# RWKV mixer: the planner counts TensorE's operands as ready 0.3 later than their end

## The chip, the cores and the metric

One NeuronCore of a Trainium2 chip runs the whole program. The metric is the device time of one execution in microseconds; of the kernel before three runs are shown. TensorE is called PE here, VectorE DVE, ScalarE ACT, GpSimd POOL, and SP is the queue that issues most DMAs. PE's granted clock is either 1.00 (2.4 GHz) or 0.50 (1.2 GHz) in the profile.

## What is computed

A trunk of two layers over 256 tokens of width 2048, in float32. Layer 0 is attention plus a Mamba-2 mixer, layer 1 an RWKV-7 mixer, and each is followed by a squared-ReLU MLP. The change touches layer 1's mixer alone. Cut to what matters:

```python
r = xr @ w_r;  k = xk @ w_k;  v = xv @ w_v            # 2048 x 2048 each
a = sigmoid(a0 + (xa @ a1) @ a2);  g = sigmoid(xg @ g1) @ g2
def step(S, inp):                                     # one head, one token
    r_t, w_t, k_t, v_t, a_t, b_t = inp
    sa = einsum('bhvk,bhk->bhv', S, a_t)
    S = S * w_t[:, :, None, :] + sa[..., None] * b_t[:, :, None, :] + v_t[..., None] * k_t[:, :, None, :]
    return S, einsum('bhvk,bhk->bhv', S, r_t)
y = group_norm(y) * ln_w + ln_b + bonus;  out = (y * g) @ w_o
```

## The kernel before

**Layout.** Activations stand with channels on the 128 partitions and the 256 tokens along the free axis. A projection of 2048 to 2048 is cut into 16 output tiles of 128 (units), each over 16 k tiles. For accuracy each weight tile is split into a rounded part hi (ACT) and a rest lo (DVE), so that one k tile costs three matmuls on PE: hi with the rounded input, hi with the input's rest, lo with the rounded input. The text calls these three a **triple**. In the order of PE's instructions a triple is two rows, `pu<-S?,hi ... x2` and `pu<-S?,lo`, with SA or SB as the input.

**The RWKV mixer** (`mixer1`) runs over 16 pairs of heads. The recurrence is done in four chunks of 64 tokens, and each pair is a set of stages, each a chain of short steps over PE, DVE, ACT and POOL:

- `prep_a` (PE: `ps_a`, the low-rank products) and `prep_b` (PE: `ps_b`) make the scaled keys and queries; small transfers (`dn`, `Nb`) spread diagonal blocks, and `substitute` inverts them on POOL.
- `values` reads a unit of the projection v out of its PSUM bank (PE: `pu<-rk`, `pu<-cst,v`). The bank is free for the next unit only after that. There are two such banks.
- `levels` builds an inverse of 64 by 64 from those of 16: four PE steps, `ps_i<-X,NT`, `ps_i<-Pm,Xt`, `ps_i<-X,NT`, `ps_i<-Xt,P`, each of which needs what DVE (or ACT) made of the one before.
- `chunks` carries the state over four chunks. In each, PE does `ps_c<-uv,AR`, then DVE copies `rhs`, PE does `ps_c<-rhs,YY`, ACT writes `uv`, PE does `ps_c<-uv,bkn` and `ps_y<-uv,G`, and DVE updates the state for the next chunk.
- `finish` normalises on DVE and POOL, transposes on PE (`ps_y<-cst,yc`), and `mixed` splits the result on ACT and DVE into SB (pairs 0 to 7) or SA (pairs 8 to 15), the input of the output projection.

**What sets the order.** Every engine executes its instructions in the order written. A planner in the kernel's Python, the class `Streams`, writes that order: it holds every stage and the feed of projections (`load`, `halve`, `project` in `feed`) as sequential programs, knows a rough duration of each operation, and issues next the operation that can start first. `start` (L238) computes that: for PE it is the later of the time when PE is free and the time when the operands are there, plus the load of the first stationary operand. A triple of the projection has its operands long before, so it can start whenever PE is free. The feed issues its parts in a fixed list; the last are four parts that need the mixed heads: three with SA (units `+0`, `+1`, `+2` of the output projection, where k tile 15 needs pair 15) and one with SB. After `mixer1` comes `out_proj`, written in plain order, which does the rest of the output projection. SP issues the weights' loads, three tiles ahead, and the small transfers, and its order comes from the same planner.

Of the kernel before, what the change touches and what calls it, by code (L numbers as in the profile page):

```python
# [6 lines left out]
F32R = mybir.dt.float32r  # L7
# [6 lines left out]
P = 128  # L14
# [11 lines left out]
# ---------------------------------------------------------------- host layout  # L26

# order of the 64 channels of a rotary head: each 32-partition quadrant holds 16
# frequencies of the first half followed by the same 16 of the second half
ROPE = np.concatenate([np.arange(0, 16), np.arange(32, 48), np.arange(16, 32), np.arange(48, 64)])  # L30
# query heads of an output tile: one of an even and one of an odd key/value head
# [50 lines left out]
for _k, _v in CONST.items():  # L82
    _l = int(_k in ("triu", "cos", "sin", "amask"))     # the second array serves layer 0 alone
    COFF[_k] = (_l, NCONST[_l], _v.shape[1])
    NCONST[_l] += _v.shape[1]


def _units(w):
    """[K, M] -> [M/128, 128, K/128, 128]"""
    k, m = w.shape  # L90
    return np.ascontiguousarray(w.reshape(k // P, P, m // P, P).transpose(2, 1, 0, 3))
# [6 lines left out]
def _heads(v):  # L98
    """a column to a head, on the first 64 partitions"""
    return np.concatenate([v.reshape(-1, HD).T, np.zeros((HD, D // HD), np.float32)], 0)  # L100


def layout(inp):
# [7 lines left out]
        np.arange(3584, 4096),            # B, C  # L111
        np.arange(2560, 3584),            # x
        np.arange(1280, 1536), kcols,     # v, k
        qcols,
        np.arange(1536, 2560),            # z
# [43 lines left out]
# ---------------------------------------------------------------- interleaving  # L159
# [4 lines left out]
def eP(cost, after=None, shape=WIDE):  # L164
    """shape: the time to load the first stationary operand, which the matmul before hides, and the
    last matmul's time, which hides the next load"""
    return "P", cost, after, shape
# [22 lines left out]
# the order of the parts of the projections and the weights by which Streams chooses  # L190
# [5 lines left out]
def prm(n, d):  # L196
    return PRM.setdefault(n, d)


class Streams:  # L200
    count = -1
    """Issues the operations of several sequential programs in one order for every engine.

    A program is a generator; before an operation it yields the engine, a rough duration (us) and the
    time its operands are there (default: when its last operation ends), or the events it has to
    follow (which no later operation of it starts before). The operation that can start first is
    issued next."""
    LAT = {"P": 0.2, "D": 0.13, "A": 0.15, "G": 0.1, "S": 2.3}

    def __init__(self):  # L210
# [7 lines left out]
        self.dma = 0.0  # L218

# [15 lines left out]
    def stream(self, g, bias=0.0, lasting=False):  # L235
        """lasting: may still run when run() returns"""
        self.heads.append([g, None, 0.0, bias, 0.0, lasting])

    def start(self, h):
        """when the operation at the head of a program can start"""  # L240
# [9 lines left out]
        if op[0] == "P":  # L250
            load = op[3][0]
            return max(self.free["P"] + max(0.0, load - self.tail), t + load - 0.07)
        return max(self.free[op[0]], t)

    def transfer(self, t, n):
        """when a load of n columns that could end at t at the earliest ends"""
# [3 lines left out]
    def run(self):  # L260
        """until the programs that aren't lasting are done"""
# [27 lines left out]
class Part:  # L289
    """Some k tiles of a unit, a 128-wide output tile of a projection. tiles: where the halves of the  # L290
    weights come to stand if the feed shall only split them; ready: the events that X[:, k] (the tiles) wait for"""
# [5 lines left out]
class Turns:  # L297
    """Tiles of a pool, n to a name, in turn"""
# [11 lines left out]
# ---------------------------------------------------------------- the program  # L310

class Trunk:
# [4 lines left out]
    # -- small helpers ---------------------------------------------------  # L317
# [34 lines left out]
    def split(self, dst, src):  # L352
        """dst F32R [.., 512]: the rounded value and what it leaves, exactly"""
# [3 lines left out]
    def rsqrt(self, pool, v, shape, tag):  # L357
        """v f32 SBUF (any compact shape) -> 1/sqrt(v), Newton from the exponent trick"""
# [11 lines left out]
    # -- a 128-wide output tile of x @ W: [128, 512] in PSUM, the sum of its  # L370
    #    two halves is the product ------------------------------------------
# [20 lines left out]
    # -- 1/rms of the tokens --------------------------------------------------  # L392
# [8 lines left out]
    def token_rstd(self, acc, n, out_bc, pspool, tag):  # L401
        """acc: squares summed over tiles [128 ch, 256]; -> 1/rms [128 t, 2], and on all partitions in out_bc"""
# [17 lines left out]
    # -- projections as streams -------------------------------------------  # L420
    def even(self, t):
        """whether Pool should take what could start at t"""
# [3 lines left out]
    def feed(self, sch, parts, pool=None, step=1, bias=(0.1, 0.0), also=(), lasting=False):  # L426
        """Loads, splits and multiplies parts in their order. A unit's product stands in sums[unit] at
        ("sum",) + unit, and its reader has to set ("out",) + unit; parts with tiles of their own end with
        ("w", key) and their reader sets ("used", key). pool(t): whether Pool takes the low halves, step: k tiles
        issued at once; both can be changed in sch. also: (i, event, tile, source), loads behind the one of part i"""  # L430
# [77 lines left out]
    # -- squared-ReLU MLP ------------------------------------------------------  # L508
    def norm_split(self, k, x, gname, X):
        """X[:, k] = split(x * g)"""  # L510
# [4 lines left out]
    def mlp(self, l, x, X, U, acc, finish, end=NK):  # L515
        """end: the output tiles from there on lack the last quarter of the hidden units"""
# [21 lines left out]
    # -- layer 0: attention and SSD ---------------------------------------------  # L538
    def rsqrt_steps(self, pool, v, tag):
        """rsqrt as steps of a stream"""  # L540
# [15 lines left out]
    def rstd_steps(self, acc, n, out_bc, pspool, pool, tag):  # L556
        """token_rstd as steps of a stream, from several partial sums"""
# [20 lines left out]
    def mixer0(self, x, X, Y, early):  # L578
        """early: the output tiles to which the attention heads are added ahead of the SSD heads"""
# [3 lines left out]
        with tc.tile_pool(name="m0", bufs=1) as m0, tc.tile_pool(name="m0t", bufs=1) as mt, \  # L583
# [9 lines left out]
            # the projections, in the order of their use  # L593
# [6 lines left out]
            # the input goes between the first weights, the constants behind it  # L600
# [5 lines left out]
            # the norm of the input  # L606
# [12 lines left out]
            def squares(k):  # L619
                """on ACT and DVE or on Pool, a sum to each"""  # L620
# [50 lines left out]
            def steps(_):  # L671
                """the time steps, their decays and the sums of those"""
# [15 lines left out]
                # softplus = max(v, 0) + log1p(exp(-|v|)), log1p(e) = 2 atanh(e / (2 + e))  # L688
# [38 lines left out]
            # B, C, x: causal convolution, SiLU  # L727
# [25 lines left out]
            # SSD  # L753
# [7 lines left out]
            def shared(_):  # L761
                """what the heads of a group share"""
# [72 lines left out]
            # attention  # L835
# [5 lines left out]
            def rope(dst, u, n=None, ns=None):  # L841
                """n: the weights of a norm, ns: with its halves exchanged"""
# [17 lines left out]
            def heads(j):  # L860
                """values and keys, then queries"""
# [52 lines left out]
            def attn(i, j):  # L914
# [34 lines left out]
                # the transposed probabilities, normalised  # L949
# [26 lines left out]
            # the gate and its group norm  # L976
# [52 lines left out]
    def out_proj(self, w, Y, x, finish, part=None, early=NK, ahead=0):  # L1029
        """part: what the first half of the rows of w has given (all of them for the first ahead tiles); it is in x  # L1030
        already for the first early tiles"""
# [12 lines left out]
    # -- layer 1: RWKV-7 time mixing ---------------------------------------------  # L1044
# [677 lines left out]
```

## Time and profile before

| | us |
|---|---|
| runs | 2529.85, 2542.24, 2548.86 (median 2542.24) |
| profiled execution, span (the page gives no other time of it) | 2551.5 |
| PE busy over the span | 2477.5 (97%) |
| DVE busy | 1738.2 (68%) |
| ACT busy | 1306.5 (51%) |
| POOL busy | 527.2 (21%) |
| HBM traffic over the span | 162 GB/s |
| the pairs of heads, 1320 to 1761 us: span, PE busy | 441.00, 424.64 |

Busy time is the union of an engine's instructions. For PE it is a modelled end, so a busy PE can still run at half its clock; the granted clock of a stretch has to be read beside it. A wait that a row of the timeline shows in brackets is time in which the engine stood still before the instruction, and the name behind the arrow is what it waited for.

### The profile page before, as it was taken

To read this page: it belongs to the slowest core of one execution; us is meant where nothing else is said; L and a number is where in the kernel's file an instruction comes from. 1 tells how busy PE (TensorE), PEld (TensorE's weight loads), DVE (VectorE), ACT (ScalarE), POOL (GpSimd) and SP (SyncE) were. 2 spreads that over 40 slices of the span, in tenths; PEclk is the share of its full clock that TensorE was granted. 3 is DMA by queue.
4 is the path that set the end of the run, shared out by engine and by line. 5 is a ranking of instruction groups with operands and counts; after the bars stand their busy time and mean duration, and the time that the engine had idled before them with its cause. 6 is when DMAs were issued, how large, how long until landed. Compare 5 with 4: busy or idle time off the path is not lost. (4 is left out here: it accounts for less than half of the span.)

```text
span 2551.5 us, 45990 instructions
## 1 busy us (share of the span) xinstructions
PE 2477.5 (97%) x17612; PEld 2181.3 (85%) x17612; DVE 1738.2 (68%) x3287; ACT 1306.5 (51%) x2398; POOL 527.2 (21%) x933
## 2 busy tenths in 40 slices
PE   8999999999999999979999999999899999999999
PEld 7988988888888888879998888788688888888887
DVE  7888876656656656679876767667665565665665
ACT  5455555435445345556656566555453453453543
POOL 3443200000000000046455656552200000000000
PEclk9999999999999999989999999899999999999999
DMA  5433455555555555634442323334455555555554
GB/s 193 141 108 109 151 187 182 187 185 188 184 189 184 188 184 188 209 113 164 162 153 93 108 95 106 97 108 171 145 190 186 187 184 188 185 188 185 189 194 162
DMA packets 130348, 415.27 MB, mean 163 GB/s; under 512 B 23600, under 2 KB 26288, under 8 KB 130128
## 3 DMA queue, kind: packets, MB, share of 16 engines
q1 hardware_dynamic: 128160, 406.44, 46.9%
q0 software_dynamic: 1968, 5.90, 0.6%
q8 instruction: 138, 2.26, 0.3%
q14 instruction: 82, 0.67, 0.1%
HBM read 407.56 MB, written 4.72 MB: 162 GB/s over the span
## 5 line engine op out<-in xcount | busy, mean ns | idle before, releaser
L322 DVE TENSOR_TENSOR lo<-wt,hi 128x1024 fp32r<-128x1024 f32 (+2 forms) x895 | 937.4, 1054 | 529.6 <-ACT hi L319 511.8
L319 ACT ACTIVATE hi<-wt 128x1024 fp32r<-128x1024 f32 (+2 forms) x945 | 813.6, 873 | 818.3 <-PE pu L343 786.7
L343 PE MATMUL pu<-SA,hi 128*128 128x512 f32 (+2 forms) x4184 | 1162.0, 349 | 18.2 <-ACT SA L319 8.0
L343 PE MATMUL pu<-SB,hi 128*128 128x512 f32 (+2 forms) x3304 | 1003.1, 366 | 4.0 <-POOL SB L322 2.2
L343 PE MATMUL pu<-SA,lo 128*128 128x256 f32 (+1 forms) x3168 | 895.8, 283 | 0.3 <-DVE lo L322 0.3
L343 PEld LDWEIGHTS pu<-SA,hi 128*128 128x128 f32 (+1 forms) x4184 | 724.8, 191 | 135.2 <-ACT hi L319 9.7
L343 PE MATMUL pu<-SB,lo 128*128 128x256 f32 x2752 | 775.7, 282 | 1.7 <-DVE lo L322 1.6
L343 PEld LDWEIGHTS pu<-SB,hi 128*128 128x128 f32 (+1 forms) x3304 | 587.0, 190 | 115.6 <-POOL SB L322 2.6
L343 PEld LDWEIGHTS pu<-SA,lo 128*128 128x128 f32 (+1 forms) x3168 | 603.6, 191 | 1.2 <-DVE lo L322 0.5
L343 PEld LDWEIGHTS pu<-SB,lo 128*128 128x128 f32 x2752 | 522.6, 190 | 2.5 <-DVE lo L322 2.3
L1694 POOL DMA_DIRECT2D out<-xT x16 | 8.7, 544 | 708.0 <-DVE xT L322 708.0
L1661 POOL DMA_DIRECT2D xd<-xh x13 | 7.2, 554 | 696.5 <-DVE xh L322 696.5
L322 DVE TENSOR_TENSOR xh<-xh,pu 128x256 f32<-128x256 f32 x164 | 69.2, 422 | 53.7 <-PE pu L343 51.1
L322 DVE TENSOR_TENSOR xT<-xT,pu 128x256 f32<-128x256 f32 x154 | 64.8, 421 | 47.9 <-PE pu L343 45.3
L322 POOL TENSOR_TENSOR lo<-wt,hi 128x512 fp32r<-128x512 f32 (+1 forms) x50 | 69.1, 1387 | 66.3 <-ACT hi L319 62.2
L322 POOL TENSOR_TENSOR xt<-Nb,X 128x60 f32<-128x60 f32 (+14 forms) x240 | 74.7, 311 | 28.4 <-DMA Nb<-dn 12.1
L322 POOL TENSOR_TENSOR X<-X,xt 128x60 f32<-128x60 f32 (+14 forms) x240 | 74.2, 309 | 16.4
L319 ACT ACTIVATE uv<-ps_c,n 64x64 f32<-64x64 f32 x128 | 39.5, 309 | 53.0 <-PE ps_c L343 40.3
L322 POOL TENSOR_TENSOR SB<-st,SB 128x256 fp32r<-128x256 f32 x44 | 49.3, 1135 | 43.8 <-ACT SB L319 31.4
L340 DVE SCALAR_TENSOR_TENSOR uw<-u,rb 128x256 f32<-128x256 f32 x128 | 54.5, 425 | 4.4
L340 DVE SCALAR_TENSOR_TENSOR st<-dx,vec,xh 128x256 f32<-128x256 f32 x80 | 53.3, 700 | 2.0 <-POOL SB L322 2.0
L322 DVE TENSOR_TENSOR u<-pu,eb 128x256 f32<-128x256 f32 x128 | 53.6, 418 | 0.0
(310 smaller groups left out, 2073.2 us busy)
## 6 DMA issues: line engine op xcount, KB each, us to landing
wt<-in_w_up SPq DMA_DIRECT2D x256, 512.0 KB
wt<-in_w_dn SPq DMA_DIRECT2D x256, 512.0 KB
wt<-in_w_in SPq DMA_DIRECT2D x64, 512.0 KB
wt<-in_w_out SPq DMA_DIRECT2D x32, 512.0 KB
wt<-in_w_k SPq DMA_DIRECT2D x32, 512.0 KB
wt<-in_w_v SPq DMA_DIRECT2D x32, 512.0 KB
wt<-in_w_o SPq DMA_DIRECT2D x32, 512.0 KB
wt<-in_w_r SPq DMA_DIRECT2D x26, 512.0 KB
```

The source lines that it names most:

```text
L319: return self.nc.scalar.activation(out=out, in_=in_, func=func, **kw)
L322: return (eng or self.nc.vector).tensor_tensor(out=out, in0=a, in1=b, op=op)
L340: return self.nc.vector.scalar_tensor_tensor(out=out, in0=a, scalar=s, in1=b, op0=op0, op1=op1)
L343: return self.nc.tensor.matmul(out, lhsT, rhs, start=start, stop=stop)
L1661: spill = lambda d, e=nc.gpsimd: e.dma_start(out=xd[:, d, :], in_=x[d])
L1694: store = lambda d: nc.gpsimd.dma_start(out=ap["out"][:, d, :], in_=x[d])
```

## The change

`start` adds a new attribute `slack` to the time at which a PE operation's operands count as there. It is 0.0 when the planner is made, and 0.3 (the planner's unit is a rough us) from the start of `mixer1`. Nothing is computed in another way: the same instructions are issued in another order. The diff also drops comments and texts in quotes, and one added line shifts the line numbers (L343 becomes L344). Its core:

```diff
@@ class Streams @@
         self.tail = WIDE[1]
         self.dma = 0.0
+        self.slack = 0.0
...
         t = h[2] if op[2] is None else max(op[2], h[4])
         if op[0] == "P":
             load = op[3][0]
-            return max(self.free["P"] + max(0.0, load - self.tail), t + load - 0.07)
+            return max(self.free["P"] + max(0.0, load - self.tail), t + load - 0.07 + self.slack)
         return max(self.free[op[0]], t)
...
@@ mixer1 @@
                 sch.stage(whole, self.ahead)
+                sch.slack = 0.3
                 sch.pool, sch.step, sch.bias = (...)
                 sch.run()
```

What it does to the order, on PE, at three places.

**Place 1**, the third pair, from `ps_c<-uv,bkn` of its first chunk to `ps_c<-uv,AR` of its second. Before:

```order
L343 MATMUL ps_c_12608<-uv_11961,bkn_12467 64x64 x2
L343 MATMUL ps_y_12607<-uv_11961,G_12468 64x64 x2
L343 MATMUL pu_236<-SB,hi_164 128x256 x2
L343 MATMUL pu_236<-SB,lo_165 128x256
L343 MATMUL pu_236<-SB,hi_164 128x256 x2
L343 MATMUL pu_236<-SB,lo_165 128x256
L343 MATMUL ps_c_12608<-uv_11961,AR_11796 64x64 x2
```

Now, on PE at the same place:

```order
L344 MATMUL ps_c_12613<-uv_11958,bkn_12471 64x64 x2
L344 MATMUL ps_y_12612<-uv_11958,G_12472 64x64 x2
L344 MATMUL pu_119<-SA,hi_126 128x256 x2
L344 MATMUL pu_119<-SA,lo_127 128x256
L344 MATMUL pu_119<-SA,hi_126 128x256 x2
L344 MATMUL pu_119<-SA,lo_127 128x256
L344 MATMUL pu_119<-SA,hi_126 128x256 x2
L344 MATMUL pu_119<-SA,lo_127 128x256
L344 MATMUL pu_236<-SB,hi_164 128x256 x2
L344 MATMUL pu_236<-SB,lo_165 128x256
L344 MATMUL ps_c_12613<-uv_11958,AR_11796 64x64 x2
```

Between two steps of a chain there are four triples where there were two.

**Place 2**, the 14th pair, from the second step of `levels` on. On PE before:

```order
L343 MATMUL ps_i_12480<-Pm_12472,Xt_12471 32x32 x16
L346 MATMUL pu_236<-cst,v_11962 64x128 x4
L343 MATMUL ps_b_11960<-AR_11797,bk_11909 128x128 x4
L343 MATMUL ps_i_12480<-X_12470,NT_11799 32x32 x8
L343 MATMUL pu_119<-SB,hi_164 128x256 x2
L343 MATMUL pu_119<-SB,lo_165 128x256
L343 MATMUL pu_119<-SB,hi_164 128x256 x2
L343 MATMUL pu_119<-SB,lo_165 128x256
L343 MATMUL ps_i_12480<-Xt_12471,P_12555 32x32 x8
L343 MATMUL pu_236<-SB,hi_239 128x256 x2
```

Now, on PE, up to the first steps of `chunks` of that pair:

```order
L344 MATMUL ps_i_12474<-Pm_12465,Xt_12464 32x32 x16
L344 MATMUL ps_y_12612<-uv_11958,G_11956 64x64 x2
L344 MATMUL ps_i_12474<-X_12463,NT_11799 32x32 x8
L344 MATMUL pu_236<-rk_11939,rkb_11961 128x256
L344 MATMUL ps_i_12474<-Xt_12464,P_12559 32x32 x8
L347 MATMUL pu_236<-cst,v_11959 64x128 x4
L344 MATMUL ps_c_12613<-uv_12196,AR_11795 64x64 x2
L344 MATMUL ps_c_12613<-rhs_12621,YY_11802 64x64 x2
L344 MATMUL pu_236<-SB,hi_239 128x256 x2
```

No triple is left between these steps: the projections have run on to the point where they need the PSUM bank that `values` (`pu_236<-rk`, `pu_236<-cst,v`) has to clear first. With the rows ahead of it this run has 21 rows of the mixer without a triple; there is one more such run, of 12 rows, at the first chunks of the second pair.

**Place 3**, the end: pair 15's last step of `chunks`, its transposes, and the first output unit that needs it. On PE before (21 triples stand between the first and the second row of the mixer):

```order
L343 MATMUL ps_y_12864<-uv_12199,G_11959 64x64 x2
L343 MATMUL pu_236<-SB,hi_164 128x256 x2
L343 MATMUL pu_236<-SB,lo_165 128x256
...
L343 MATMUL pu_236<-SB,lo_127 128x256
L346 MATMUL ps_y_12864<-cst,yc_12859 64x128 x4
L343 MATMUL pu_236<-SB,hi_126 128x256 x2
```

Now, on PE:

```order
L344 MATMUL pu_119<-SA,lo_165 128x256
L344 MATMUL ps_y_12892<-uv_12196,G_11956 64x64 x2
L347 MATMUL ps_y_12892<-cst,yc_12906 64x128 x4
L344 MATMUL pu_119<-SA,hi_164 128x256 x2
L344 MATMUL pu_119<-SA,lo_165 128x256
```

The 21 triples ahead of the transposes and the nine behind them have moved to earlier places; the `pu_119<-SA` row behind the transposes is already k tile 15 of unit `+0`, which needs pair 15 to be mixed.

## Rows read from the trace of the kernel before

**Rows 1.** The page: span of the profiled execution.

```profile
span 2551.5 us, 45990 instructions
```

**Rows 2.** Busy time by stretch: PE, PEld, DVE, ACT, POOL (instructions), granted clock, DMA share, GB/s.

```profile
1320.00:1761.00 441.00, 424.64 (x4914) 362.71 (x4912) 310.02 (x928) 262.38 (x659) 257.55 (x623) 0.95 0.34 110
...
1320.00:1370.00 50.00, 48.21 (x565) 41.72 (x564) 30.85 (x91) 26.80 (x67) 32.08 (x88) 0.90 0.40 119
1370.00:1420.00 50.00, 47.78 (x559) 40.75 (x560) 37.25 (x113) 29.02 (x75) 30.18 (x64) 0.93 0.32 103
1420.00:1470.00 50.00, 47.46 (x557) 40.26 (x556) 35.17 (x109) 27.76 (x70) 33.96 (x86) 0.93 0.30 97
...
1620.00:1670.00 50.00, 47.14 (x497) 39.43 (x495) 34.20 (x107) 25.74 (x64) 24.79 (x57) 0.80 0.28 89
```

**Rows 3.** PE's waits, 1320 to 1761: total us, times, longest.

```profile
PE ps_i L343 <- DVE Pm L322: 3.0, 4, 1.4
PE ps_i L343 <- DVE P L1502: 3.0, 4, 1.0
```

**Rows 4.** PE's timeline, waits in brackets: start, us, instruction; last, one stretch.

```profile
1328.05 0.45 PE L343 MATMUL ps_i<-X,NT 32*32 32x32 f32 x32 [1.24 <-DVE X L1473]
...
1330.18 0.65 PE L343 MATMUL ps_i<-Pm,Xt 32*32 32x32 f32 x32 [0.44 <-DVE Pm L322]
...
1384.44 0.34 PE L343 MATMUL ps_c<-uv,AR 128*64 128x64 f32 x4 [0.80 <-DVE uv L337]
...
1622.80 0.45 PE L343 MATMUL ps_i<-Pm,Xt 32*32 32x32 f32 x32 [0.52 <-DVE n L337]
...
1624.98 0.44 PE L343 MATMUL ps_i<-X,NT 32*32 32x32 f32 x16 [0.47 <-DVE X L322]
...
1627.71 0.44 PE L343 MATMUL ps_i<-Xt,P 32*32 32x32 f32 x16 [0.96 <-DVE P L1502]
...
1629.24 0.63 PE L346 MATMUL pu<-cst,v 128*64 128x128 f32 x4 [0.53 <-DVE bv L322]
...
1630.00:1650.00 20.00, 20.00 (x111) 16.83 (x108) 8.18 (x25) 8.05 (x21) 9.63 (x32) 0.50 0.16 46
```

**Rows 5.** PE's timeline: the steps of one pair that did not wait.

```profile
1657.79 0.45 PE L343 MATMUL ps_i<-Pm,Xt 32*32 32x32 f32 x32
...
1659.44 0.44 PE L343 MATMUL ps_i<-X,NT 32*32 32x32 f32 x16
...
1660.71 0.44 PE L343 MATMUL ps_i<-Xt,P 32*32 32x32 f32 x16
...
1662.17 0.33 PE L343 MATMUL ps_c<-uv,AR 64*64 64x64 f32 x4
...
1663.33 0.33 PE L343 MATMUL ps_c<-rhs,YY 64*64 64x64 f32 x4
```

**Rows 6.** PE's timeline at the mixer's end, and tile lo there: PE, PEld, DVE.

```profile
1748.34 0.34 PE L343 MATMUL ps_y<-uv,G 128*64 128x64 f32 x4
...
1756.27 0.60 PE L346 MATMUL ps_y<-cst,yc 128*64 128x128 f32 x4
...
1760.78 0.85 PE L343 MATMUL pu<-SA,hi 128*128 128x256 f32 x2 [0.69 <-ACT SA L319]
...
1748.70:1756.27 7.57, 5.79 (x21) 4.03 (x21) 3.77 (x6) 0.00 (x0) 1.00 1.00 364
```

**Rows 7.** PE's timeline: a triple behind a mixer step, then one behind a triple.

```profile
1716.70 0.51 PE L343 MATMUL pu<-SB,hi 128*128 128x256 f32 x2
...
1717.17 0.40 PE L343 MATMUL pu<-SA,hi 128*128 128x256 f32 x2
...
1717.52 0.40 PE L343 MATMUL pu<-SA,hi 128*128 128x256 f32 x2
```

**Rows 8.** Busy time by stretch: the output projection's start.

```profile
1761.00:1830.00 69.00, 57.61 (x330) 48.88 (x330) 50.10 (x96) 32.07 (x54) 18.85 (x12) 0.98 0.42 145
```

## Prediction, written before the changed kernel ran

> **What bounds the kernel now.** I read the page first for the span [rows 1], then busy time by stretch for the only stretch whose order changes, then PE's waits in it, then PE's timeline around them. The pairs of heads take 441.00 us, 17% of the span, and PE is busy for 424.64 us of it [rows 2]. So PE is the bound there, and the same matmuls are issued before and after. The stretch can shorten only by what PE loses in it, and there are two losses. PE stands still for 441.00 - 424.64 = 16.4 us, in 28 waits. Nearly all are for DVE, in `levels` and `chunks` [rows 3], and none names a DMA. And its clock is granted at 0.90, 0.93, 0.93 and 0.80 in four of the 50 us stretches [rows 2]: 5.0 + 3.5 + 3.5 + 10.0 = 22.0 us lost. Everything that the change can give lies in these 38 us, 1.5% of the span. What it can take away is not bounded so.
>
> **The change, part by part.** The planner now puts a triple ahead of a mixer step whose operands would come within 0.3 after PE is free. Counted in both orders over the 208 gaps between successive steps of `levels` and of `chunks`, 359 triples stood in them and 437 stand there now.
>
> *Waits between steps.* The first two waits (1.24 and 0.44 us) stand at a place where the order is nearly as it was, so they stay; the last (0.69) belongs to the end [rows 4, 6]. That leaves 25 waits and 16.4 - 2.4 = 14.0 us, 0.56 each. Place 1 shows the best case: its 0.80 us wait [rows 4] gets two more triples, 0.71 us at 0.35 each [rows 7]. But one wait in three has no more cover than before, for instance the 0.96 us one [rows 4]. The planner's 0.3 on each would be 25 x 0.3 = 7.5 us. The ends are 0 (DVE's own queue, with the weights' lo in it, makes the operands late and they stay late) and 14.0. I take -7.5, half way, since the added triples per gap (0.375 x 0.35 = 0.13 us) are few but most stand at the gaps that waited.
>
> *Two runs of mixer steps without a triple.* Here the projections wait for a PSUM bank, so DVE's time is bare. At place 2, from the second step of `levels` to the first of `chunks`, 1657.79 to 1662.17 = 4.38 us passed where PE never waited [rows 5], so the chain needs at most that when DVE is free. PE has six steps there now, at 0.33 to 0.45 us each [rows 5], some 2.1 us: up to 2.3 us idle. The next step followed after 1.16 us [rows 5]; one step of 0.33 covers it: 0.8 more. That is 3 us for the lower end. Where DVE was loaded, 1622.80 to 1629.24 = 6.44 us went by [rows 4]: 2.1 more. The steps ahead of it and the shorter run at the second pair I put at 0 to 3 together, an estimate by the waits of 0.5 to 0.96 [rows 4]. Ends 3 and 8.2; I take +6, nearer the loaded row, since DVE is busy 70% of the stretch [rows 2].
>
> *The end.* Before, from the last `ps_y<-uv,G` to k tile 15 of unit `+0`, 1748.34 to 1760.78 = 12.44 us pass, and 30 triples hide all but 0.69 of it [rows 6]. Now nothing stands there but the transposes. Less the two PE steps' own 0.34 and 0.60, 11.5 us are bare. DVE spends 3.77 us of that on lo halves [rows 6], which the new order issues ahead of or behind the chain; part of this fell while ACT or POOL had the chain, so I take half off: 9.6 us idle. The wait that was there goes: +8.9. Ends: all the lo off (+7.0), none off (+10.8). Nothing behind it makes this good: `out_proj` cannot split more than three weight tiles ahead, and PE is already idle for 69.00 - 57.61 = 11.4 us of its first 69 [rows 8].
>
> *Changes between triples and mixer steps.* A triple behind a mixer step takes 1717.17 - 1716.70 = 0.47 us, one behind a triple 0.35 [rows 7]. The projections stand in 225 runs where there were 237: 12 x 0.12 = -1.4 us, 0 to -1.4.
>
> *The clock.* The 0.50 stretch from 1630 follows four waits of 0.47 to 0.96 us within 7 us [rows 4]. Of the four losses the first follows the two waits that stay, so I keep 5.0. Of the other 17.0 I let half go with half of the waits: -8.5, between 0 and -17.0. Place 2 gets a stretch of its own: +3.5 like the 0.93 rows, 0 to 10 like the 0.80 row [rows 2]. The idle end adds one too, in a stretch where PE is busy 83% [rows 8]: +3, 0 to 6. Together -2.0. Beside this rule of thumb from rows stands one of the Trainium skill (TensorE: Matmul & The Clock Gate, section Why this matters for your kernels): it asks for no long PE-idle gap between bursts of matmuls if the clock is to hold mid-kernel. This trace does not bear that out, as no wait ahead of the 1630 stretch is over 0.96 us; by that rule the sum would be the third rival's.
>
> *Nothing for the rest.* Loads and small transfers on SP, and steps on ACT and POOL, change places by a few rows. DMA is busy 0.34, ACT 262 and POOL 258 of 441 us [rows 2], so there is room; if `substitute` on POOL came late, `levels` would be next, and that is in the waits' ends. The MLPs' order is unchanged.
>
> **Sum:** -7.5 + 6 + 8.9 - 1.4 - 2.0 = **+4.0 us**. The profiled execution, 2551.5 us, would be 2555.5; it lies 0.4% above the median of the runs, which I move by the same amount: 2542.2 + 4.0 = **2546**. The gain is real, but the order takes its cover from the end, where it hid twelve microseconds.
>
> **Rivals.** 1 (faster): the waits nearly vanish (-12), and with them the three later clock losses (-17.0) while no new one comes; the uncovered places cost their lower ends (3 and 7.0). -12 + 3 + 7.0 - 1.4 - 17.0 = -20.4: 2522. For it: clock losses are larger than waits here. Against it: eight or more us idle at the end have not been seen to pass without a loss of clock in this stretch.
>
> 2 (slower): the bank at place 2 decides. If DVE is loaded there, its 8.2 us bring a stretch at 0.50 as long as that from 1630 (+10), the end costs 10.8 and 6 of clock, and the waits, shortened by 3 only, keep their clock losses: -3 + 8.2 + 10.8 - 1.4 + 16 = +30.6: 2573. It decides from about 6 us of idle there. Against it: the waits would have to keep most of their length though 78 triples stand between the steps.
>
> 3: the clock does not answer to short waits, only to the long idle at the end. Then no loss is spared and one is added (+6): -7.5 + 6 + 8.9 - 1.4 + 6 = +12: 2554. For it stands only the skill's rule named above; the trace speaks against it.
>
> 4: the change moves rows but not waits. DVE works its queue in order, so a late operand stays late behind a lo, and the triple only shifts which step waits: 0 + 6 + 8.9 - 1.4 - 2.0 = +11.5: 2554. For it: eleven of the thirteen kinds of wait name DVE. Against it: PE would have 0.13 us more work per gap on the mean.
>
> **How the numbers follow.** About 1% (25 us) is what a measurement of this kernel tells from no change. Chances: forecast 0.62, rival 1 0.12, rival 2 0.09, rival 3 0.10, rival 4 0.07. Faster by over 1% (under 2517) needs rival 1 and a little more: 0.03, and 0.01 from the forecast's edge: 0.04. Slower by over 1% (above 2568): two thirds of rival 2 and 0.01 of the others: 0.07. Within 1%: 0.89. The range takes in the forecast with its bounds and rivals 3 and 4, and leaves out most of rivals 1 and 2: 2527 to 2563.
>
> **What would show it.** Right: PE's waits named Pm, P, uv and X fall to about half in total; one wait of 5 to 7 us ahead of the last `ps_y<-cst,yc` and one of about 4 us for SA behind it; waits at the 14th pair's `levels` that add up to 4 us or more; a granted clock below 1.00 right behind the end. Wrong: no wait over 3 us at the end, which would mean that my reading of the order there is false; or the waits between steps undiminished (rival 4); or a clock of 1.00 from the third pair on (rival 1).

## The result, and the profile after

The changed kernel took 2556.9 us (median of 13 runs, 2545.5 to 2564.3), the kernel before 2539.2 (13 runs, 2527.4 to 2549.8): a ratio of 1.0061 with a 95% interval of 1.0039 to 1.0083, or some 15.5 us more by the means of the runs (the medians lie 17.7 apart). That is slower, and less than the 1% that was set as the bound. The forecast had the sign, the range and the case (within 1%); its +4.0 was too small by 11 us, and the section on why shows that one of its terms had the wrong sign.

The page of the kernel after, for [rows 1]: its span and its engines' busy time.

```profile
span 2562.6 us, 45974 instructions
PE 2476.5 (97%) x17612; PEld 2179.5 (85%) x17612; DVE 1741.9 (68%) x3287; ACT 1308.4 (51%) x2398; POOL 534.9 (21%) x933
```

PE is busy as long as before (2477.5) and the span is 11.1 us longer: PE stands still. Busy time by stretch of the kernel after, with the columns of [rows 2]:

```profile
1320.00:1370.00 50.00, 46.86 (x669) 39.29 (x667) 34.44 (x99) 28.49 (x72) 30.99 (x83) 1.00 0.36 110
1370.00:1420.00 50.00, 48.11 (x511) 41.82 (x508) 40.38 (x118) 32.02 (x80) 36.69 (x81) 1.00 0.36 108
1420.00:1470.00 50.00, 48.46 (x589) 40.89 (x589) 37.39 (x108) 30.47 (x77) 31.58 (x74) 1.00 0.34 108
1470.00:1520.00 50.00, 47.82 (x528) 40.88 (x526) 33.28 (x101) 27.19 (x69) 24.65 (x59) 0.83 0.28 91
...
1620.00:1670.00 50.00, 45.87 (x548) 39.03 (x548) 37.71 (x113) 30.90 (x77) 31.17 (x69) 0.90 0.34 109
...
1720.00:1770.00 50.00, 40.17 (x437) 33.95 (x437) 27.52 (x83) 25.96 (x66) 17.54 (x40) 0.92 0.40 138
```

The first three stretches, which before ran at 0.90 to 0.93, are at 1.00 now; lower clocks have come later, from 1470 on and at the end. These are single executions, and run 6 below shows how far the clock moves between two of the same kernel. PE's waits in the kernel after, 1320 to 1775 (total us, times, longest), for [rows 3]:

```profile
PE ps_y L347 <- POOL yc L323: 5.9, 2, 5.3
PE ps_i L344 <- DVE X L323: 4.3, 7, 1.3
PE pu L347 <- DVE bv L323: 4.0, 4, 2.1
PE ps_i L344 <- DVE P L1503: 3.8, 6, 1.2
PE ps_c L344 <- DVE rhs L1540: 3.4, 6, 1.4
PE pu L344 <- ACT SA L320: 3.3, 1, 3.3
PE ps_c L344 <- DVE uv L338: 1.5, 1, 1.5
PE ps_i L344 <- DVE Pm L323: 1.4, 2, 0.8
```

In the kernel before, beside Pm and P [rows 3]:

```profile
PE ps_c L343 <- DVE uv L337: 2.3, 4, 0.8
PE ps_i L343 <- DVE X L1473: 1.6, 2, 1.2
...
PE ps_i L343 <- DVE X L322: 1.2, 2, 0.7
PE pu L346 <- DVE bv L322: 0.7, 2, 0.5
```

Of the four names in the prediction only Pm (3.0 to 1.4) and DVE's uv (2.3 to 1.8) fell. P rose from 3.0 to 3.8 and X from 2.8 to 5.1 (each name with all its rows). bv rose from 0.7 to 4.0, rhs from 1.5 to 3.4, and 1.9 us of waits for an uv of ACT are new. All waits from the first `ps_i<-X,NT` to the output projection add up to 31.3 us, for 16.1 before. The end, on PE's timeline of the kernel after, for [rows 6]:

```profile
1764.91 1.06 PE L347 MATMUL ps_y<-cst,yc 128*64 128x128 f32 x4 [5.26 <-POOL yc L323]
1769.32 1.04 PE L344 MATMUL pu<-SA,hi 128*128 128x256 f32 x2 [3.34 <-ACT SA L320]
...
1770.37 0.63 PE L344 MATMUL pu<-SA,hi 128*128 128x256 f32 x2
...
1771.01 0.63 PE L344 MATMUL pu<-SA,hi 128*128 128x256 f32 x2
```

8.6 us idle where 0.69 was, and half clock with it: the transposes take 1.06 us for 0.60, triples come every 0.64 us for 0.35 [rows 6, 7]. Place 2 on the same timeline:

```profile
1680.17 0.44 PE L344 MATMUL ps_i<-X,NT 32*32 32x32 f32 x16 [0.49 <-DVE X L323]
...
1681.42 0.44 PE L344 MATMUL ps_i<-Xt,P 32*32 32x32 f32 x16 [0.18 <-DVE P L1503]
1682.66 0.62 PE L347 MATMUL pu<-cst,v 128*64 128x128 f32 x4 [0.80 <-DVE bv L323]
...
1684.99 0.48 PE L344 MATMUL ps_c<-rhs,YY 64*64 64x64 f32 x4 [1.44 <-DVE rhs L1540]
```

With 0.27 and 0.21 just ahead this stretch without a triple costs 3.4 us, the shorter one at the second pair 1.1.

### Why the waits between steps did not fall

I followed each of the 288 pairs of successive steps of `levels` and `chunks` through both orders and both timelines. 139 pairs got more triples between them (188 before, 411 now). Five of these pairs waited before, 2.1 us together, and all five waits are gone. But of the waits at such steps only these five got more cover: of the other 15 before, eight (5.0 us) have as many triples as they had and seven (4.8 us) have fewer. Place 1 is one of the five: its 0.80 us [rows 4] have no bracket any more in the kernel after.

```profile
1377.00 0.34 PE L344 MATMUL ps_c<-uv,AR 128*64 128x64 f32 x4
...
1379.07 0.33 PE L344 MATMUL ps_c<-rhs,YY 64*64 64x64 f32 x4 [0.57 <-DVE rhs L1540]
```

But the next step waits there now, and it is one of eleven pairs that got more triples, did not wait before and wait now: 8.0 us in all. More cover, and yet a wait, since the operand comes later than the cover lasts. Less cover is no better guide: the 79 pairs that lost triples (200 to 74) waited 4.8 us before and wait 3.6 now. The ninth pair's last step of `levels` shows it. Before, it followed 1.35 us behind the step before it (1542.59 to 1543.94) with one triple between them and no wait. After, three triples stand between them and 2.85 us pass, on PE and DVE of the kernel after:

```profile
1541.92 0.44 PE L344 MATMUL ps_i<-X,NT 32*32 32x32 f32 x16
...
1542.54 0.38 DVE L338 TENSOR_SCALAR gs<-va 128x4 int32<-128x4 int32 x1
1542.84 0.41 DVE L341 SCALAR_TENSOR_TENSOR ka<-ta,ka 128x256 f32<-128x256 f32 x1
1543.17 0.65 DVE L338 TENSOR_SCALAR gy<-gs 128x4 int32<-128x4 int32 x1
1543.85 0.53 DVE L323 TENSOR_TENSOR gt<-gy 128x4 f32<-128x4 f32 x1
1544.41 0.30 DVE L1503 COPY P<-ps_i 32x128 f32<-32x128 f32 x1
...
1544.77 0.41 PE L344 MATMUL ps_i<-Xt,P 32*32 32x32 f32 x14 [0.71 <-DVE P L1503]
```

DVE never stops. The copy to P, which PE waits for, stands behind another pair's `finish` (gs, gy, gt) and a `ka`. The slack moves PE's rows, but what decides is how DVE's single queue interleaves the chains, and that changed with it. It is the same in all eleven: the DVE instruction that PE waits for starts within 0.04 us of the end of the one ahead of it. And through all 31 waits for DVE in this stretch (20.0 of the 31.3 us) DVE has no pause of 0.1 us or more; before, that held for 25 of 26 (14.4 of 16.1 us). The longest of them, 2.06 us for bv at 1631.06, is not at a step of a chain but at the PSUM bank that `values` clears; bv stood behind 18 instructions that DVE had worked through without such a pause since 1623.59.

Two of the three longest of the eleven have one thing more: a DVE instruction that takes far longer than usual. On DVE, POOL and PE of the kernel after:

```profile
1479.50 1.28 POOL L323 TENSOR_TENSOR ll<-wt,lh 128x512 fp32r<-128x512 f32 x1 [0.70 <-ACT lh L320]
1479.54 1.79 DVE L323 TENSOR_TENSOR lo<-wt,hi 128x512 fp32r<-128x512 f32 x1
1481.36 0.30 DVE L1503 COPY P<-ps_i 32x128 f32<-32x128 f32 x1
1481.71 0.44 PE L344 MATMUL ps_i<-Xt,P 32*32 32x32 f32 x16 [1.19 <-DVE P L1503]
```

A lo usually takes 0.69 us. This one starts 0.04 us behind POOL's `ll` and takes 1.79. The same stands at 1598.45 (1.77 us, and a wait of 1.32). The Trainium skill (SBUF — State Buffer, section Who interferes with whom) says that a VectorE instruction with two inputs in SBUF and a GpSimd instruction that reads SBUF exclude each other, so that the later one waits for the earlier one's end; these rows agree. Run 11 below measures its price.

### The profile page after: what moved, and what is told of

Same layout as the page of the kernel before. It is cut to its first block, busy times and chain, and to the rows that moved or that the text cites. A ratio compares the mean times of both kernels' runs of the same rounds, so it can differ in the third digit from the quotient of the medians.

```text
span 2562.6 us, 45974 instructions
## 1 busy us (share of the span) xinstructions
PE 2476.5 (97%) x17612; PEld 2179.5 (85%) x17612; DVE 1741.9 (68%) x3287; ACT 1308.4 (51%) x2398; POOL 534.9 (21%) x933
## 4 chain that ended last, share of the span: by engine, by line
PE 82%; DVE 10%; issue 4%; POOL 2%; ACT 1%; DMA 1%; SPq 0%; POOLq 0%; DVEq 0%; ACTq 0%
PE pu L344 74%; DVE lo L323 2%; PE ps_c L344 2%; PE ps_b L344 1%; PE ps_y L344 1%; PE ps_a L344 1%; PE ps_t L344 1%; DVE st L341 1%; POOL xT L323 1%; DVE AR L323 0%; PE ps_i L344 0%; PE ps_b L347 0%; PE ps_y L347 0%; DVE xT L323 0%; DVE acc L323 0%
## 5 line engine op out<-in xcount | busy, mean ns | idle before, releaser
L344 PE MATMUL pu<-SA,hi 128*128 128x512 f32 (+2 forms) x4184 | 1163.0, 349 | 19.4 <-ACT SA L320 9.8
L344 PE MATMUL pu<-SB,hi 128*128 128x512 f32 (+2 forms) x3304 | 1001.2, 366 | 4.4 <-POOL SB L323 2.2
L344 PE MATMUL pu<-SA,lo 128*128 128x256 f32 (+1 forms) x3168 | 896.1, 283 | 0.3 <-DVE lo L323 0.3
L344 PEld LDWEIGHTS pu<-SA,hi 128*128 128x128 f32 (+1 forms) x4184 | 724.8, 191 | 136.6 <-ACT SA L320 10.6
L344 PE MATMUL pu<-SB,lo 128*128 128x256 f32 x2752 | 775.6, 282 | 1.7 <-DVE lo L323 1.7
L344 PEld LDWEIGHTS pu<-SB,hi 128*128 128x128 f32 (+1 forms) x3304 | 587.8, 190 | 116.1 <-POOL SB L323 2.6
L344 PEld LDWEIGHTS pu<-SA,lo 128*128 128x128 f32 (+1 forms) x3168 | 603.3, 190 | 1.5 <-DVE lo L323 0.5
L344 PEld LDWEIGHTS pu<-SB,lo 128*128 128x128 f32 x2752 | 522.5, 190 | 2.3 <-DVE lo L323 2.1
L323 POOL TENSOR_TENSOR SB<-st,SB 128x256 fp32r<-128x256 f32 x44 | 48.8, 1124 | 44.3 <-ACT SB L320 32.0
```

Source lines behind the costliest of these rows:

```text
L323: return (eng or self.nc.vector).tensor_tensor(out=out, in0=a, in1=b, op=op)
L344: return self.nc.tensor.matmul(out, lhsT, rhs, start=start, stop=stop)
```

## The experiments

Each ratio is of means, to runs of the kernel before beside it on the same chip, with its 95% interval; the intervals of some 0.2% are 5 us either way. Run 6, the kernel before once more, has no row. The waits are those of the profiled execution, from the mixer's first `ps_i<-X,NT` to the output projection, as far as the last `ps_y<-uv,G` and behind it.

| kernel | ratio to before | us against before | waits before + behind the last `ps_y<-uv,G` |
|---|---|---|---|
| before | 1 | 0 | 15.4 + 0.7 |
| after | 1.0061 [1.0039, 1.0083] | +15.5 | 22.7 + 8.6 |
| 1 end kept | 1.0057 [1.0037, 1.0078] | +14.5 | 19.1 + 3.0 |
| 2 k tile 15 first | 1.0047 [1.0029, 1.0066] | +12 | 22.0 + 6.2 |
| 3 end only | 1.0057 [1.0038, 1.0076] | +14.5 | 17.1 + 8.6 |
| 4 less lo, before's order | 0.9915 [0.9891, 0.9938] | -21.6 | 4.7 + 0.8 |
| 5 less lo, after's order | 0.9989 [0.9970, 1.0007] | -3 | 12.5 + 8.6 |
| 7 slack -0.15 | 1.0048 [1.0027, 1.0069] | +12 | 15.6 + 2.6 |
| 8 every 4th lo on POOL | 1.0064 [1.0037, 1.0091] | +16 | 20.9 + 2.1 |
| 9 every 3rd lo on POOL | 1.0095 [1.0064, 1.0127] | +24 | 23.5 + 2.2 |
| 10 every 6th, planned | 1.0069 [1.0035, 1.0102] | +17.5 | 19.9 + 4.9 |
| 11 ll cut, after's order | 1.0036 [1.0008, 1.0063] | +9 | 18.9 + 8.6 |
| 12 ll cut, before's order | 0.9983 [0.9951, 1.0015] | -4 | 13.6 + 0.8 |

**1. The slack without its end.** It is 0 again once the 12th pair's `chunks` are issued, so that the stretch without a triple at place 2 goes too.

```diff
-            return max(..., t + load - 0.07 + self.slack)
+            return max(..., t + load - 0.07 + (0.0 if ("chunks", 11) in self.done else self.slack))
```

> The slack of 0.3 holds only until the chunks of pair 11 (of 0 to 15) are issued, then it is 0 again: on PE 22 triples stand again between the last ps_y<-uv,G and its transposes (0 in the changed kernel, 21 before), and the order up to there is the changed kernel's. My theory: half or more of the loss is the uncovered end. Its waits of 5.3 and 3.3 us shrink to under 1.5 together and the clock stays at 1.00 there, so 8 + 3 us of the changed kernel's +15.5 us go: +2 to +6 us against the kernel before. Rival A (the end's wait is made good behind it, and the loss is in the waits between steps): +12 to +15 stays. Rival B (the clock's losses are chance and the waits are all of it): +5 to +8.

On PE's timeline of this run the wait ahead of the transposes is gone and 2.98 us stay:

```profile
1763.25 0.60 PE L347 MATMUL ps_y<-cst,yc 128*64 128x128 f32 x4
1767.19 0.87 PE L344 MATMUL pu<-SA,hi 128*128 128x256 f32 x2 [2.98 <-ACT SA L320]
```

5.6 us less idle than after at the end, yet 2560.2 us and as slow as after. The expectation (+2 to +6) failed: nearly all of the loss comes without most of the end's wait. Its runs lose 45 us to the clock on the mean and before's beside them 31, by the reckoning in the section on why.

**2. K tile 15's input part moved in the feed's list.** `o15a` goes ahead of the units `+0` to `+2`.

```diff
-'o14a', '+0a', '+1a', '+2a', 'o15a'
+'o14a', 'o15a', '+0a', '+1a', '+2a'
```

> The changed kernel with one entry of the feed's list moved: unit o15 (8 triples, needs only SB) stands ahead of the three units with SA instead of behind them. On PE 8 triples come to stand behind the last ps_y<-uv,G, 8 x 0.35 = 2.8 us. My theory: the wait ahead of the last transposes falls from 5.3 to 2.3 to 2.6 us and everything behind moves up by as much: +12 to +13 us against the kernel before instead of +15.5, a little less if the clock also holds. Rival A (the end's wait is made good behind it): no change, +15 to +16. Order effects on the steps between: none expected, as the order ahead of the last steps is the same.

The wait ahead of the transposes is nearly halved (2.81 us, for 2.3 to 2.6 expected), the one for SA is not:

```profile
1751.42 0.85 PE L347 MATMUL ps_y<-cst,yc 128*64 128x128 f32 x3 [2.81 <-POOL yc L323]
...
1755.82 1.04 PE L344 MATMUL pu<-SA,hi 128*128 128x256 f32 x2 [3.34 <-ACT SA L320]
```

2556.1 us against before's 2543.9 beside it, +12, as expected. But the interval overlaps that of after's +15.5, so a gain of some 3 us is not shown.

**3. The end alone.** The slack is 0 until the 15th pair's `chunks` are done, then 0.7.

```diff
-            return max(..., t + load - 0.07 + self.slack)
+            return max(..., t + load - 0.07 + (0.7 if ("chunks", 14) in self.done and self.slack else 0.0))
```

> The kernel before up to the last pair; only once the chunks of pair 14 are issued is the slack 0.7. On PE no triple then stands between the last ps_y<-uv,G and its transposes, as in the changed kernel, and the order of the rest of the mixer is the old one. My theory: the end's two waits (5.3 and 3.3 us) and a clock loss of 3 to 4 us come by this alone: +8 to +13 us against the kernel before. Rival A (made good behind it): 0 to +3. Rival C (the changed kernel's loss comes from the steps between alone): 0.

```profile
1767.03 1.06 PE L347 MATMUL ps_y<-cst,yc 128*64 128x128 f32 x4 [5.22 <-POOL yc L323]
...
1771.43 1.04 PE L344 MATMUL pu<-SA,hi 128*128 128x256 f32 x2 [3.34 <-ACT SA L320]
```

The end's idle time comes back whole (5.22 and 3.34) with a mixer that is otherwise before's, and the time is +14.5, a little over the +8 to +13 expected. So the end alone is enough for nearly all of the loss, and by run 1 the rest alone is enough too. The waits add up (6.0 more in run 1, 9.6 in run 3, 15.2 in after); the times do not.

**4 and 5. Less of DVE's work on the lo halves**, in before's order and in after's. Run 4 also leaves `+ self.slack` out of `start`; the rest of the edit is the same.

```diff
+                    if sch.slack and not g:
+                        q = slice(q.start, q.start + 128)
                     self.sub(lo[:, q], c[:, q], hi[:, q].bitcast(F32), nc.gpsimd if g else None)
```

> The kernel before in its own order; in the pairs of heads DVE makes only the first 128 of every 512 columns of the weights' lo halves (the rest is left out, so the projections there are not the reference's). DVE's lo steps take about 0.25 us each in place of 0.69 to 0.76, some 50 us less of its 310. Theory D (DVE works its queue in order, and a step of the chain stands behind a lo or another pair's steps): PE's waits ahead of the last ps_y<-uv,G fall from 15.4 us to under 9, and with them the 0.50 stretches: -5 to -12 us against the kernel before. Theory L (a step's own latency from PE to DVE and back is the wait): waits stay at 14 to 16 us and the time within 3 us.

> The changed kernel in its own order, with the same columns of lo left out. Theory D: the waits ahead of the last ps_y<-uv,G fall from 22.7 us to under 12, most of the four to six 0.50 stretches between 1330 and 1700 go, and what is left against the shortened kernel before is the end: its two waits stay at 8 to 9 us together. Against the kernel before: 0 to +8; against the shortened one before: +8 to +13. Theory L: waits stay at 20 us or more and the time at +12 to +16 against the kernel before.

A stretch of run 4 (columns of [rows 2]):

```profile
1620.00:1670.00 50.00, 48.78 (x599) 40.98 (x597) 32.06 (x116) 31.12 (x80) 29.58 (x83) 1.00 0.34 110
```

In before's order the waits fall from 16.1 to 5.5 us, none over 0.82, and the clock is 1.00 in all nine stretches from 1320 to 1770. 21.6 us are gained of the 38 that the prediction named as all there is, more than theory D's 5 to 12. In after's order the waits fall by 10 us as well (to 12.5 ahead of the last `ps_y<-uv,G`; theory D said under 12), and the time is -3 where it said 0 to +8. But the long ones stay: bv 2.06, rhs 1.34 for 1.44, yc 5.25 for 5.26, SA 3.34. They are not the lo's doing; for bv and rhs DVE was at work on other steps throughout in the kernel after. The two orders differ by some 19 us with the lighter DVE, where theory D had 8 to 13, and by 15.5 with the full one, so relieving DVE does not save the change.

**6. The kernel before once more**, to see its clock in another execution.

> The kernel before once more, for a second look. PE's waits in the pairs of heads should be the same to 1 us (16.4 in all). The profile on which the forecast rests had a mean granted clock of 0.983, where the plain runs beside it have 0.983 to 0.992: if the 0.50 stretches come by where the waits fall in time, this look shows fewer or shorter ones with the same waits, 10 to 18 us lost there instead of 22. If they are fixed by the order, the same four stretches with 22 us come again.

2543.1 us. The waits are the same (15.2 us), but its stretches at half clock between 1320 and 1780 are two of 10.2 and 13.7 us, where the execution behind [rows 2] had four of 44.3 us together. The stretch that stood at 0.80 [rows 2] is at 1.00 here:

```profile
1620.00:1670.00 50.00, 47.65 (x543) 40.19 (x532) 38.59 (x120) 32.30 (x83) 34.22 (x83) 1.00 0.34 110
```

So half of what I called the clock loss of before belonged to that execution, not to the order.

**7. The other direction**: the slack is -0.15, so triples give way to mixer steps.

```diff
-                sch.slack = 0.3
+                sch.slack = -0.15
```

> The other direction: the slack is -0.15 in the pairs of heads, so mixer steps go ahead of triples that would start up to 0.15 later. Between successive steps of levels and of chunks stand 292 triples (359 before, 437 with 0.3), and 23 triples behind the last ps_y<-uv,G (21 before, 0 with 0.3). If triples between the steps are what keeps PE from waiting, its waits rise from 15.4 to 20 to 25 us: +5 to +12 us. If DVE's queue makes the operands late whatever stands between (theory D), the waits stay within 3 us of the old ones and the time within 4 us.

+12 us, with 15.6 us of waits in the mixer, where the first theory had 20 to 25 and theory D a time within 4 us. At the end PE waits 2.63 us for SA at 1752.98. So both theories missed. Waits of 2.1 us more do not make 12 us. Two more parts can be read. On the mean the runs lose 37 us to the clock, before's beside them 33. And PE's own work got longer: its busy time from the first `ps_i<-X,NT` to the wait for SA, without what half clock adds, is 401.6 us here (408.44 busy, 6.83 lost to the clock), and 395.6 to 398.2 in the traces of before and of runs 3, 4, 6 and 12, which all have before's order in the mixer. Two more triples ahead of that wait are 0.7 of these 3 to 6 us; where the rest comes from was not found.

**8 to 10. The lo halves partly on POOL**, in search of a faster kernel. In 8 and 9 (the first part of the diff, with 3 in place of 4 in run 9) the planner is not told, so PE's order is before's; in 10 (the last line) it is. The slack is 0 in all three.

```diff
+                    if sch.cnt is not None:
+                        sch.cnt.append(0)
+                        g = g or len(sch.cnt) % 4 == 0
                     self.sub(lo[:, q], c[:, q], hi[:, q].bitcast(F32), nc.gpsimd if g else None)
...
+                sch.pool = lambda t: sch.cnt.append(0) or len(sch.cnt) % 6 == 0
```

> The order of before on PE, with every fourth lo half of the mixer's projections made on POOL in place of DVE, of which the planner is told nothing. That takes 32 x 0.744 = 24 us from DVE and gives POOL 32 x 1.35 = 43 us (the row of ll on POOL), 258 to about 300 of 450 us. Theory (DVE's time for the lo halves is what most of the waits and the lost clock of before hang on): leaving out 128 x 0.417 = 53 us of it gave -21.6 us, so 24 us give about -10: 0.993 to 0.998 of before, PE's waits in the mixer from 15 to about 10 us. Rival (the waits only go over to POOL, which does the substitution and the centring in its own order): between 0 and +10 us, with X, xt and yc as POOL's names in the waits.

> As the run with every fourth, but every third lo half on POOL: 43 x 0.744 = 32 us from DVE, 43 x 1.35 = 58 us to POOL. Theory: -13 us, 0.992 to 0.998 of before. Rival: POOL's queue decides, and this run is slower than the one with every fourth, +5 to +20 us against before.

> slack 0.0, every sixth lo half of the mixer's projections on POOL, and the planner told of it, so that the order changes too: 351 triples in the 208 gaps for 359, 18 for 21 at the end, two short runs of mixer steps without a triple (11 and 13 rows). DVE loses 21 x 0.744 = 16 us. Theory: -6 us, and about +3 for the two runs: -3. Rival (any new order costs the clock that before's order happens to keep): +5 to +12 us.

All three are slower, as the rivals said, and by more than they said: +16 for 0 to +10, +24 for +5 to +20, +17.5 for +5 to +12. By name nearly all waits stay with DVE (X, P, Pm) and not with POOL. But the longest of run 8 is POOL's all the same. On POOL, DVE and PE of that run:

```profile
1326.72 1.26 POOL L324 TENSOR_TENSOR lo<-wt,hi 128x512 fp32r<-128x512 f32 x1
...
1329.02 0.29 DVE L324 TENSOR_TENSOR Xt<-X,cst 128x128 f32<-128x128 f32 x1 [4.57 <-POOL X L324]
...
1329.72 0.65 PE L345 MATMUL ps_i<-X,NT 32*32 32x32 f32 x32 [2.48 <-DVE X L1478]
```

A lo stands in POOL's queue ahead of the last step of `substitute`, and DVE itself stands idle until POOL has made X. In run 8 the waits in which DVE was at work throughout are 15.5 us for 14.4 before, so most of what is new there goes back to POOL or the end; in run 9 they are 20.4. And DVE itself became slower. Groups of instructions of run 8, 1320 to 1770 (busy us, mean ns):

```profile
L324 DVE TENSOR_TENSOR lo<-wt,hi 128x512 fp32r<-128x512 f32 x99 | 75.5, 771 | 20.0 <-ACT hi L321 19.2
L342 DVE SCALAR_TENSOR_TENSOR bk<-ka,Lc 64x256 f32<-64x256 f32 x28 | 20.7, 739 | 0.4
```

The 31 lo halves on POOL take 1343 ns each. Before, the same stretch has DVE's `lo` at 748 ns and `bk` at 583. With every third lo on POOL they are at 829 and 751.

**11 and 12. POOL's `ll` in four pieces.** The same work, in instructions of 128x128.

```diff
-                    self.sub(lo[:, q], c[:, q], hi[:, q].bitcast(F32), nc.gpsimd if g else None)
+                    cut4 = range(q.start, q.stop, 128 if g and sch.cut else n)
+                    for o in cut4:
+                        q = slice(o, o + (128 if g and sch.cut else n))
+                        self.sub(lo[:, q], c[:, q], hi[:, q].bitcast(F32), nc.gpsimd if g else None)
```

> The order of after; POOL makes each 128x512 rest ll of the low-rank weights in the mixer as four instructions of 128x128 in place of one of 1.28 us. In after the four waits behind a DVE instruction that started under such an ll and took 1.22 to 1.79 us are 1.19 (Xt,P at 1481.71), 1.32 (X,NT at 1600.60), 0.78 (rhs at 1578.87) and 0.57 us (bv at 1457.97). Theory (DVE stands still until POOL's instruction has ended, and that, which the planner does not count, makes the longest waits outside the two runs): DVE's lo no longer takes over 1.3 us there, these four shrink from 3.9 to about 1.5 us, and with the clock behind them the time falls by 3 to 8 us against after: 1.003 to 1.005 of before. Rival (what is late is the place in DVE's queue; one blocked instruction makes no difference): 1.006, with the four waits within 0.3 us of what they were in total.

> The same cut of ll, in the order of before. Three waits of before stand behind a DVE instruction that started under an ll: 0.65 (rhs at 1604.19), 0.52 (Pm at 1622.80) and 0.49 us (X at 1539.57). Theory: they go, 1.7 us, and the time falls by 1 to 5 us: 0.998 to 1.000 of before. Rival: 1.000, or above it by POOL's extra time for three more instructions a piece (12 x 3 x 0.05 = some 2 us, off the path).

In run 11 the wait of 1.19 us has become 0.35, on the timelines of POOL, DVE and PE (compare 1479.50 above):

```profile
1469.73 2.34 POOL L324 TENSOR_TENSOR ll<-wt,lh 128x128 fp32r<-128x128 f32 x4 [0.71 <-ACT lh L321]
1469.77 0.97 DVE L324 TENSOR_TENSOR lo<-wt,hi 128x512 fp32r<-128x512 f32 x1
1470.77 0.30 DVE L1507 COPY P<-ps_i 32x128 f32<-32x128 f32 x1
1471.12 0.44 PE L345 MATMUL ps_i<-Xt,P 32*32 32x32 f32 x16 [0.35 <-DVE P L1507]
```

The four waits named in advance went from 3.86 to 1.11 us (1.19 to 0.35, 1.32 to 0.50, 0.78 to 0.26, 0.57 to none), the mixer's waits from 22.7 to 18.9, and the ratio from 1.0061 to 1.0036. The waits' part of the theory is shown. The time, 6 us better, is where the theory put it, though the two intervals still overlap. Now POOL pays: its `ll` takes 2.34 us for 1.28. In before's order two of the three waits named went (0.52 and 0.49) and the one for rhs stayed (0.64 for 0.65); the gain, -4 us, can't be told from none. So no version here is shown to beat before with all of the work done.

## Why the prediction was right, and where it was not

| term | forecast | read from the traces |
|---|---|---|
| waits between steps | -7.5 | +2.9 (22.7 less 4.4 in the two runs is 18.3, for 15.4) |
| two runs without a triple | +6 | +4.4 (3.4 and 1.1) |
| the end | +8.9 | +7.9 (5.26 + 3.34 - 0.69) |
| changes of kind | -1.4 | -1.3 (PE's busy time without what half clock adds: 395.6 to 394.4) |
| clock | -2.0 | -2.7 in the two profiled executions (half clock under PE's busy time, 22.0 to 19.3); some +9 by all runs, of which some 4.5 fall into idle time that the waits have already |
| sum | +4.0 | +11.2 by these terms of the profiled executions, +15.5 by the runs |

The terms are read between the first `ps_i<-X,NT` and the wait for SA. The two profiled executions there, before and after (columns of [rows 2]):

```profile
1328.05:1760.78 432.73, 417.61 (x4858) 356.05 (x4858) 305.40 (x920) 258.46 (x651) 250.53 (x605) 0.95 0.33 108
```

```profile
1324.76:1769.32 444.56, 413.68 (x4855) 352.08 (x4855) 309.67 (x920) 258.48 (x651) 255.88 (x606) 0.95 0.33 106
```

That is 11.8 us longer, for 11.1 over the whole execution. Half clock costs 22.2 us of the first and 24.1 of the second, but in the second 4.8 of it pass while PE stands idle anyway.

- **The bound held.** PE's work is the same to 1.3 us, and the loss lies in PE's waits and clock in the pairs of heads. Run 4 took 21.6 of the 38 us by removing most of the waits and all of the half clock there.
- **The end held**: a wait of 5.26 us ahead of the transposes (5 to 7 forecast), 3.34 for SA (about 4), 8.6 for 9.6 in all, and half clock with it. Nothing behind made it good: from the matmul that waits for SA on, 790.8 us are left before and 793.3 after. One reason in it was wrong: the lo halves on DVE add nothing to the wait, as run 5 with the lighter lo has the same 5.25.
- **The two runs without a triple held** within their ends (3 to 8.2): with 4.4 us nearer to the unloaded chain, not to the loaded row that I chose. That row's 6.44 us end at the step for v; to the same step as in the free row it is 7.00 (1629.80). The sign named, 4 us or more in the 14th pair's `levels`, did not come: 3.4 in all, and only 0.7 of it in `levels`. The lo halves were not what counted there either, since run 5 has 1.34 of the 1.44 us.
- **The waits between steps failed, by 10 us.** The sign named for it did not come: Pm, P, uv and X did not halve but went from 11.1 to 12.1 us (those for DVE). The sign of being wrong did: the waits between steps are undiminished. Two steps of the working were false. The first could have been read from the order: I wrote that one wait in three had no more cover and that most of the added triples stood at the gaps that waited, but only 5 of the 20 waits at such steps, 2.1 us, got more. The second: I took the slack off each wait and left the operands' times alone. Waits that got triples did vanish (2.1 us to none), but eleven new ones came (8.0 us), because DVE's queue, in another interleaving, makes other operands late. That is the fourth rival's mechanism, and its 2554 us was the nearest of the prices, with the third's; I gave it 0.07, arguing from the mean cover per gap, which is no argument about a queue. About 2.2 of the 2.9 us sit behind POOL's `ll` (3.9 us there now, 1.7 before). With POOL's `ll` cut, runs 11 and 12 still have 14.7 us (outside the two stretches without a triple) against 13.6, so no fall either way.
- **The clock was mis-sized.** The time that a run loses to its clock is its span times what its mean clock lacks to 1. It is 42 us on the mean of after's runs and 31 to 35 of before's in the four sets of runs that have its clock, so some 9 us more. I worked from one profiled execution of before whose loss was 43 us (its span, 2551.5 us, is longer than any of the 13 runs took), and credited the change with half of a loss that before does not usually have. In the two profiled executions the term even came out at -2.7; that is chance. Rival 3's rule of the Trainium skill (TensorE: Matmul & The Clock Gate, section Why this matters for your kernels) is not borne out as a sole cause: before lost clock with no wait over 1.42 us, and run 4, which has fewer of these short waits (none over 0.82 us), keeps 1.00. But at an idle stretch of 5.2 us the clock does fall in every trace that has one (after and runs 3, 5 and 11).
- **The range held partly by luck.** It was drawn to take in rivals 3 and 4, and it is there that the time fell. Of the forecast's own sum the largest credit, the waits, has the wrong sign.
- **What stays open**: the time does not follow the sum of the waits. Runs 1 and 3 cost as much as both together, and run 7 costs 12 us with 2.1 us more waits. Lost clock (45, 38, 40 and 37 us in runs 1, 2, 3 and 7, for 31 of before beside the first three and 33 beside run 7) can make up the difference in runs 1 and 3 and part of it in run 7, and idle time at half clock counts twice in such a sum; what sets the half clock off in each was not found. Nor was a planner tried that gives DVE's steps of the chains priority over other work, which would test the queue's part directly.

## What to carry to other kernels

A planner that orders work for a busy engine also reorders the queues that feed it; before crediting slack with shorter waits, count in both orders which of the waits get more cover, and look at which instruction stands ahead of the awaited one on the feeding engine, now and after. Work that is spent as cover early is missing at the end, and that part of the price can be read from the order and one stretch of the timeline. Take the clock loss of a kernel from several executions, never from the one that was profiled.

## What the runs showed of the hardware

- A DVE instruction on two SBUF inputs that starts just behind a POOL one waits for it: `lo` took 1.77 to 1.79 us for 0.69 when it started 0.04 and 0.11 us behind an `ll` of 1.28 and 1.33, and 0.95 to 0.97 when the `ll` was cut in four. With the cut, in the mixer of runs 11 and 12, no 128x512 `lo` took over 1.24 us. POOL pays then: four pieces took 2.34 us.
- So work moved from DVE to POOL slows what stays on DVE: `bk` from 583 to 739 ns on the mean with 31 lo halves on POOL.
- The same kernel's half-clock time in one stretch was 44.3 us in one execution and 23.9 in another, with waits of 15.4 and 15.2 us.
